# A hybrid decoder layer on one core: order of the first loads and products, the engine of the low parts, a buffer for attention's last piece, transposes one step ahead, gates and table loads moved

## The chip, the cores and the metric

The kernel runs on one core of one Trainium2 chip. The time is the device time of one execution in microseconds (us); several runs are made, and their median is compared. Engines are named as the profile names them: PE (TensorE), DVE (VectorE), ACT (ScalarE), POOL (GpSimd), SP (SyncE, which here issues nearly all DMAs).

## What is computed

One layer: a norm, one projection of 1024 to 2816 columns that is cut into eight parts, three groups of heads (a diagonal complex state-space scan with GELU and a sigmoid gate, a short convolution, attention into 256 memory tokens), one output projection, a residual sum and a final norm. Sequence 2048, model width 1024, all float32.

```python
hn = _rmsnorm(h, norm_g[l])
proj = hn @ w_in[l]
(a_in, a_gate, c_in, c_b, c_c, c_gate, q, q_gate) = jnp.split(proj, split_idx, axis=-1)
y_ssm = _s5_group(a_in, ...) * jax.nn.silu(a_gate)
y_conv = _short_conv_group(c_in, c_b, c_c, ...) * jax.nn.silu(c_gate)
mem_n = _rmsnorm(mem, mem_norm_g[l])
y_mem = _memory_xattn_group(q, mem_n, w_mem_kv[l]) * jax.nn.silu(q_gate)
y = jnp.concatenate([y_ssm, y_conv, y_mem], axis=-1)
h = h + y @ w_out[l]
...
return _rmsnorm(h, final_norm_g)
```

## The kernel before

**Products in three terms.** Each operand of a large product is kept as a high part, rounded to the matrix engine's float format (`fp32r`), and a low part, what rounding left. `mm3` (its three products are lines 81, 82 and 83) adds high x high, high x low and low x high. `split` makes the parts: ACT casts the high part (line 86), and the engine that it is given subtracts for the low part (line 77, the helper `tt`). So each weight tile costs a DMA, an ACT cast, and a subtraction of 128x1024 on DVE or POOL. `wtile` does all three; its default engine is POOL (`e=G`). `proj` passes DVE, but POOL for the tile q = 2; `wout` passes POOL, and `memory_kv` takes the default. `put` and `fetch_y` give some low parts of results to POOL too, and `glu` a sum. The staging buffers of weights (`wst`) are two, so a third load waits until a cast and a subtraction are done.

**Stages.** The sequence is cut into four tiles q of 512 columns. `prep` loads four row blocks of x, sums squares (ACT), scales rows (`row_rstd` with a power on POOL, then DVE, line 602), transposes them on PE (`rows_T`, names `trq`) and splits them into `hn`. `ain`, `agate`, `qproj` and `conv` are the eight parts of the projection, 24 products of 128x512 for each 128 columns (names `psai`, `psag`, `psq`, `psqg`, `psci`, `pscc`, `pscb`, `pscg`). `ssm_prologue`, `gen_table` and `gen_turns` build the state-space tables during tile 0 and write them to DRAM; `ssm` reads them back two buffers at a time (`tb`) and does `ps_v`, a scan on DVE, and `ps_y`. `memory_kv` makes keys and values (`psk`, `psv`). `attention` does scores (`sps`), exponents on ACT (`pe`), transposes (`trp`), their split (`pT`, line 77) and the weighting (`po`, line 809). `glu` gates the state-space result, `outproj` and `outproj_last` do the output projection (`po<-wo`) and the final norm.

**Order.** The program interleaves generators with fixed rates (end of the listing), and a scheduler then reorders each engine's instructions by its own estimate, save where the program forbids it. Each engine runs its queue in order; so an instruction that waits holds up all behind it. The order in which the engines got the instructions is shown with the change.

**Lines that matter.** L602 row scaling of x, L427 to L431 the table product and its sum and copy (`Kp`), L501 and L511 the table's load and `ps_v`, L619 `gate2` (`uq`, `ua`, `uc`), L783 scores, L790 exponents, L805 to L819 the rest of attention, L131 weight loads.

```python
for h in range(2):
    ...
    for mt_ in range(2):
        ...
        split(pT[:, 0], pT[:, 1], pt.rearrange("p i c -> p (i c)"))
        for z in range(2):
            T.matmul(po, vd[:, z, mt_, 2 * j + h], pT[:, z], start=mt_ + z == 0, stop=mt_ + z == 2)
```

## Time and profile before

| | |
|---|---|
| median of 3 runs | 890.51 us (889.22 to 893.97) |
| profiled execution | 893.49 us |
| its span, first to last instruction | 891.7 us |
| mean granted clock of PE | 0.980 |
| busy PE / DVE / ACT / POOL | 834.0 / 595.1 / 391.2 / 194.3 us |
| DMA | 142.88 MB, mean 160 GB/s |

The span is that of one execution under the profiler; 1.8 us lie around it. Busy time is the time in which an engine works on instructions; PE's products overlap and their ends are modelled. An engine's idle time is put down to what released it: `psqg L81 <- DVE uq L619` reads as the product of line 81 into `psqg`, which went on when DVE had made `uq` in line 619. The granted clock is 1.00 at 2.4 GHz and 0.50 at 1.2 GHz; a stretch's mean lies between.

### The profile page before, as it was taken

What the parts mean: (1) busy time and instruction counts of PE and PEld (TensorE: products, weight loads), DVE (VectorE), ACT (ScalarE), POOL (GpSimd) and SP (SyncE); (2) the same over time, 40 slices, a digit from 0 to 9 for tenths busy, and PEclk for the clock granted to TensorE, in tenths of its full rate; (3) what the DMA queues carried; (4) which work ended last, traced back from release to release, by engine and by line L of the source; (5) the groups of instructions that cost most, each with busy time, mean ns of one, the idle gap of its engine ahead of it and who ended that gap; (6) DMA issues with size and microseconds to landing.
All of it is one profiled execution on the core that took longest, in us unless ns stands there. A gap on an engine that the chain in (4) does not pass through costs nothing. (4 is left out here: it accounts for less than half of the span.)

```text
span 891.7 us, 11628 instructions
## 1 busy us (share of the span) xinstructions
PE 834.0 (94%) x4132; PEld 685.9 (77%) x4132; DVE 595.1 (67%) x1216; ACT 391.2 (44%) x758; POOL 194.3 (22%) x113
## 2 busy tenths in 40 slices
PE   2999899869997999999999989999999999998996
PEld 1986687767886888888888867888888888776885
DVE  5898799484798597855513584426478987785363
ACT  5243433354465446534434555334354336542511
POOL 2000001130000010344435553342000011265510
PEclk9999899999998999999999999999999999999998
DMA  9563646778566342384584743466747754486361
GB/s 202 148 172 95 184 132 190 205 202 238 167 183 195 100 130 78 103 210 134 141 263 121 197 111 97 119 191 208 213 135 206 209 158 119 125 209 186 98 189 47
DMA packets 170850, 142.88 MB, mean 160 GB/s; under 512 B 41128, under 2 KB 146600, under 8 KB 170792
## 3 DMA queue, kind: packets, MB, share of 16 engines
q1 hardware_dynamic: 170792, 142.14, 56.6%
q8 instruction: 32, 0.52, 0.2%
q14 instruction: 26, 0.21, 0.1%
HBM read 113.80 MB, written 26.74 MB: 158 GB/s over the span
## 5 line engine op out<-in xcount | busy, mean ns | idle before, releaser
L77 POOL TENSOR_TENSOR wo<-wo_st,wo 128x1024 fp32r<-128x1024 f32 x26 | 66.1, 2541 | 51.8 <-ACT wo L86 50.0
L86 ACT CAST wo<-wo_st 128x1024 fp32r<-128x1024 f32 x27 | 28.2, 1045 | 40.3 <-DMA wo_st<-in_w_out_dram 16.8
L81 PE MATMUL psai<-hn,wai 128*128 128x512 f32 (+1 forms) x120 | 42.4, 361 | 2.6 <-ACT hn L86 1.6
L82 PE MATMUL psai<-hn,wai 128*128 128x512 f32 (+1 forms) x120 | 42.6, 356 | 0.1
L83 PE MATMUL psai<-hn,wai 128*128 128x512 f32 (+1 forms) x120 | 42.3, 354 | 0.0
L81 PE MATMUL psag<-hn,wag 128*128 128x512 f32 x96 | 39.3, 409 | 0.0
L81 PE MATMUL pscg<-hn,wcg 128*128 128x512 f32 x96 | 38.7, 403 | 0.0
L83 PE MATMUL pscb<-hn,wcb 128*128 128x512 f32 x96 | 37.7, 392 | 0.9 <-DVE wcb L77 0.9
L81 PE MATMUL psci<-hn,wci 128*128 128x512 f32 x96 | 38.4, 400 | 0.0
L82 PE MATMUL psag<-hn,wag 128*128 128x512 f32 x96 | 38.4, 400 | 0.0
L82 PE MATMUL pscg<-hn,wcg 128*128 128x512 f32 x96 | 38.3, 399 | 0.0
L81 PE MATMUL pscb<-hn,wcb 128*128 128x512 f32 x96 | 38.2, 398 | 0.0
L83 PE MATMUL pscg<-hn,wcg 128*128 128x512 f32 x96 | 38.2, 397 | 0.0
L81 PE MATMUL pscc<-hn,wcc 128*128 128x512 f32 x96 | 38.1, 397 | 0.0
L83 PE MATMUL psag<-hn,wag 128*128 128x512 f32 x96 | 38.0, 396 | 0.0
L83 PE MATMUL pscc<-hn,wcc 128*128 128x512 f32 x96 | 37.7, 393 | 0.3 <-DVE wcc L77 0.3
L83 PE MATMUL psci<-hn,wci 128*128 128x512 f32 x96 | 37.8, 394 | 0.0
L82 PE MATMUL psci<-hn,wci 128*128 128x512 f32 x96 | 37.6, 391 | 0.0
L82 PE MATMUL pscc<-hn,wcc 128*128 128x512 f32 x96 | 37.5, 391 | 0.0
L77 POOL TENSOR_TENSOR ymem<-uq,ymem 128x512 fp32r<-128x512 f32 x4 | 5.2, 1296 | 148.3 <-DMA wcg_st<-in_w_in_dram 132.9
L82 PE MATMUL pscb<-hn,wcb 128*128 128x512 f32 x96 | 37.5, 391 | 0.0
L77 DVE TENSOR_TENSOR hn<-trq,hn 128x512 fp32r<-128x512 f32 x32 | 21.4, 683 | 23.3 <-ACT hn L86 23.3
(704 smaller groups left out, 2582.2 us busy)
## 6 DMA issues: line engine op xcount, KB each, us to landing
wo_st<-in_w_out_dram SPq DMA_DIRECT2D x32, 512.0 KB, 3.8
tb<-t_dram SPq DMA_DIRECT2D x16, 960.0 KB, 6.1
out_dram<-h SPq DMA_DIRECT2D x32, 256.0 KB, 3.6
h<-in_x_dram SPq DMA_DIRECT2D x14, 512.0 KB, 7.2
wai_st<-in_w_in_dram SPq DMA_DIRECT2D x12, 512.0 KB, 4.2
wag_st<-in_w_in_dram SPq DMA_DIRECT2D x12, 512.0 KB, 3.9
wci_st<-in_w_in_dram SPq DMA_DIRECT2D x12, 512.0 KB, 4.1
wcc_st<-in_w_in_dram SPq DMA_DIRECT2D x12, 512.0 KB, 4.0
```

Source lines behind the costliest of these rows:

```text
L77: e.tensor_tensor(o, a, b, op)
L81: T.matmul(ps, lh, rh, start=first, stop=False, **kw)
L82: T.matmul(ps, lh, rl, start=False, stop=False, **kw)
L83: T.matmul(ps, ll, rh, start=False, stop=last, **kw)
L86: S.copy(hi, src)
```

## The change

- **Start.** `first` replaces tile 0's `prep` and its part of `ain`. Rows 0 and 1 of x come first (half of row block 0 issued from ACT), then the three weight tiles as one buffer in three loads, then rows 2 and 3 into the weights' staging buffers. `norm_g` comes as 4 KB and is spread over partitions by two products with ones. The three accumulators are filled side by side, k by k, first the columns of rows 0 and 1.
- **Low parts.** `wtile`, `wout`, `put`, `fetch_y` and the sum in `glu` use DVE; POOL keeps the powers of the row scaling and some settings of memory.
- **Row scaling** with fewer steps: sums of two halves and factors are folded into other steps. `Dg` is added to the table product by PE (24 products of 16x16 more), and one ACT copy takes it out.
- **Tables** are requested at the head of the loop over b, one step ahead. **Gates** of the query (`qgate`) come behind `agate`. Loads of the memory rows, and the first transpose of some rows, keep the program's order.
- **Attention** transposes and splits one quarter ahead of its weighting; `um` is a buffer of its own.

```diff
-    def wtile(src, rows, cols, name, e=G, dst=None, stage="w"):
+    def wtile(src, rows, cols, name, e=V, dst=None, stage="w"):
...
-        V.tensor_scalar(v, ss, 1.0 / DM, EPS, ALU.mult, ALU.add)
+        if s1 is None:
+            V.tensor_scalar(v, s0, EPS * DM, None, ALU.add)
+        else:
+            V.scalar_tensor_tensor(v, s0, EPS * DM, s1, ALU.add, ALU.add)
...
-        tt(r2, r, a, ALU.mult)
+        V.scalar_tensor_tensor(r2, r, math.sqrt(DM), a, ALU.mult, ALU.mult)
...
+                T.matmul(kp[:NH, g, 0:NH], B1[:, b * GB + gg, :], R0[:, b * GB + gg, :], start=True, stop=False)
+                T.matmul(kp[:NH, g, 0:NH], ident[:NH, :NH], Dg[:, b * GB + gg, :], start=False, stop=True)
...
-            tt(Kp[:, xs_, 7 * NH:8 * NH], kp[:NH, :, 0:NH], Dg[:, b * GB + 3 * x_:b * GB + 3 * x_ + 3, :], ALU.add)
-            V.tensor_copy(Kp[:, xs_, 8 * NH:], kp[:NH, :, NH:])
+            S.copy(Kp[:, xs_, 7 * NH:], kp[:NH])
...
         for b in range(NS):
+            if b + 1 < NS:
+                table(b + 1)
...
             if b + 1 < NS:
-                table(b + 1)
                 vmm(b + 1)
...
+    def first():
...
+        xt = [xst.tile([P, DM], F32, tag="x", name=f"x0{i}") for i in range(2)]
+        xt += [wst.tile([P, DM], F32, tag="ws", name=f"x0{i}") for i in range(2, 4)]
+        wstg = stab.tile([P, KT, WS], F32, tag="tb", name="wai_st")
...
+        ks = ((0, 2), (2, 4), (4, 8))
...
+        nc.sync.dma_start(xt[0][0:NCH], xq[0, 0, :, 0])
+        nc.scalar.dma_start(xt[0][NCH:P], xq[0, 1, :, 0])
+        for z in range(2):
+            nc.scalar.dma_start(ngr[z], norm_g[0:1, halves[z]])
+        load_x(xt[1], 0, 1)
+        for a, b in ks:
+            nc.sync.dma_start(wstg[:, a:b], w_in[0, a * P:b * P, C_AIN:C_AIN + WS].rearrange("(k p) n -> p k n", p=P))
+        load_x(xt[2], 0, 2)
...
+            T.matmul(pb, ones, ngr[z], start=True, stop=True)
+            S.copy(ng_b[:, halves[z]], pb)
...
+        def mms(z, a, b):
+            o = slice(z * 256, z * 256 + 256)
+            for k in range(a, b):
+                for t in range(3):
+                    mm3(pss[t][:, o], wa[t][:, 0, k], wa[t][:, 1, k], hn[:, 0, k, o], hn[:, 1, k, o], k == 0, k == KT - 1)
...
+        yield from rows(0)
+        yield from rows(1)
+        for a, b in ks:
+            wsplit(a, b)
+        mms(0, 0, 2)
...
+        yield from rows(3)
+        mms(1, 0, KT)
...
-        w = wtile(w_in[0, :, c0:c0 + P], DM, P, f"w{nm}{q}", G if q == 2 else V)
+        w = wtile(w_in[0, :, c0:c0 + P], DM, P, f"w{nm}{q}")
...
-        put(q, "conv", t, u_, G if t < 2 else V)
+        put(q, "conv", t, u_)
...
+        um = late["um"].tile([P, QL], F32, tag="um", name=f"um{q}{j}")
...
+        turn(0, 0)
+        yield
+        turn(0, 1)
+        weigh(0, 0)
+        yield
+        turn(1, 0)
+        weigh(0, 1)
...
-            tt(g2, f32(y_ssm[:, 0, m, :]), f32(y_ssm[:, 1, m, :]), ALU.add, G)
+            tt(g2, f32(y_ssm[:, 0, m, :]), f32(y_ssm[:, 1, m, :]), ALU.add)
...
-    def wout(q, nh, kp, dst=None, st="w", e=G):
+    def wout(q, nh, kp, dst=None, st="w"):
...
-    for _ in weave(chain(agate(0), qproj(0), conv(0, 0), conv(0, 1)), side, 1.5):
+    for _ in weave(chain(agate(0), qproj(0), qgate(0), conv(0, 0), conv(0, 1)), side, 1.5):
...
-        return chain(qproj(q), agate(q), conv(q, 0), conv(q, 1), conv(q, 2))
+        return chain(qproj(q), agate(q), qgate(q), conv(q, 0), conv(q, 1), conv(q, 2))
```

`turn(h, mt_)` does the four transposes and the split of one quarter, `weigh(h, mt_)` its two products into `po` (line 872) and, with the second, the copy and the sum into `um`.

**Order on DVE at the start**, before: the halves of row 1 (`trq_0_231`, `trq_1_238`) and, behind them, `bg`.

```order
L77 TENSOR_TENSOR hn_183<-trq_0_231,hn_183 128x4x128
L77 TENSOR_TENSOR q03a<-q03r 128x1
L77 TENSOR_TENSOR q02a<-q02a,q02v 128x1
L77 TENSOR_TENSOR wai_169<-wai_st,wai_169 128x1024
L209 TENSOR_SCALAR j_en<-j_ex 128x24
L77 TENSOR_TENSOR hn_183<-trq_1_238,hn_183 128x4x128
L77 TENSOR_TENSOR q03a<-q03a,q03v 128x1
L96 TENSOR_SCALAR q02a<-q02a 128x1
L77 TENSOR_TENSOR s_Dg<-ident,j_dd 16x384
L124 TENSOR_SCALAR bg<-bg 128x3
```

And in the change, where row 1's first half is `trq_0_226`:

```order
L95 SCALAR_TENSOR_TENSOR q02v<-ssq_363 128x1
L214 TENSOR_SCALAR j_en<-j_ex 128x24
L95 SCALAR_TENSOR_TENSOR q03v<-ssq_500 128x1
L77 TENSOR_TENSOR s_Dg<-ident,j_dd 16x384
L127 TENSOR_SCALAR bg<-bg 128x3
L215 TENSOR_SCALAR j_en<-j_en 128x24
L77 TENSOR_TENSOR q02a<-q02r 128x1
L216 TENSOR_SCALAR j_ep<-j_en 128x24
L219 SCALAR_TENSOR_TENSOR j_er<-j_en,j_ex 128x24
L77 TENSOR_TENSOR q02a<-q02a,q02v 128x1
L217 TENSOR_SCALAR j_ebits<-j_ep 128x24
L77 TENSOR_TENSOR hn_144<-trq_0_226,hn_144 128x4x128
```

The two steps that need the small loads `dd` and `bg` now stand ahead of row 1's halves.

**Order on DVE at the last row of tile 1** (row block 3, scaled in the step `xb<-xb,q13o,ng_b`; `wai` are weights of the next projection), before:

```order
L77 TENSOR_TENSOR q13o<-q13r,q13a 128x1
L77 TENSOR_TENSOR wai_2152<-wai_st,wai_2152 128x1024
L77 TENSOR_TENSOR vd<-psv_1891,vd 128x2x64
L77 TENSOR_TENSOR vd<-psv_1965,vd 128x2x64
L602 SCALAR_TENSOR_TENSOR xb_1775<-xb_1775,q13o,ng_b 128x1024
L77 TENSOR_TENSOR hn_1774<-trq_0_1951,hn_1774 128x4x128
L77 TENSOR_TENSOR hn_1774<-trq_1_1958,hn_1774 128x4x128
L77 TENSOR_TENSOR wai_2222<-wai_st,wai_2222 128x1024
```

And in the change:

```order
L77 TENSOR_TENSOR hn_1805<-trq_0_1979,hn_1805 128x4x128
L77 TENSOR_TENSOR hn_1805<-trq_1_1986,hn_1805 128x4x128
L100 SCALAR_TENSOR_TENSOR q13o<-q13r,q13a 128x1
L77 TENSOR_TENSOR wai_2254<-wai_st,wai_2254 128x1024
L77 TENSOR_TENSOR vd<-psv_1993,vd 128x2x64
L658 SCALAR_TENSOR_TENSOR xb_1806<-xb_1806,q13o,ng_b 128x1024
```

The third `wai` (`wai_2222` before, `wai_2254` now) has come from behind the row to ahead of it.

**Order on PE at the second attention piece of tile 1 and the tables** (stretch of 278 us), before:

```order
L548 MATMUL ps_y_2854<-sC_2796,tb_2719 128x128
L783 MATMUL sps_2632<-kd,qh_2415 128x256 x6
L783 MATMUL sps_2633<-kd,qh_2415 128x256 x6
L511 MATMUL ps_v_2934<-pg_2802,tb_2932 128x128 x3
L547 MATMUL ps_y_2938<-pg_2802,tb_2805 128x128
L805 MATMUL trp_2775<-ident,pe_2486 128x128 x2
L805 MATMUL trp_2845<-ident,pe_2486 128x128 x2
L81 MATMUL psag_2816<-hn_1774,wag_2813 128x512
```

And in the change, where the row of `psqg` is the last of 21 that stand there:

```order
L83 MATMUL psqg_2850<-hn_1805,wqg_2847 128x512
L842 MATMUL sps_2668<-kd,qh_2451 128x256 x6
L842 MATMUL sps_2669<-kd,qh_2451 128x256 x6
L81 MATMUL psci_2910<-hn_1805,wci_2907 128x512
L82 MATMUL psci_2910<-hn_1805,wci_2907 128x512
L83 MATMUL psci_2910<-hn_1805,wci_2907 128x512
L81 MATMUL psci_2910<-hn_1805,wci_2907 128x512
L507 MATMUL ps_v_2841<-pg_2818,tb_2821 128x128 x3
L544 MATMUL ps_y_2889<-pg_2600,tb_2698 128x128
```

Projections now stand between scores, `ps_v` and `ps_y`.

## Rows read from the trace of the kernel before

**Rows 1.** The page, busy time of PE, share of the span, instructions.

```profile
PE 834.0 (94%) x4132; PEld 685.9 (77%) x4132; DVE 595.1 (67%) x1216; ACT 391.2 (44%) x758; POOL 194.3 (22%) x113
```

**Rows 2.** PE's waits, whole span: total us, times, longest us.

```profile
PE psqg L81 <- DVE uq L619: 4.5, 1, 4.5
...
PE psv L82 <- POOL wv L77: 3.4, 1, 3.4
PE trq L144 <- DVE xb L602: 3.3, 1, 3.3
PE po L82 <- POOL wo L77: 3.0, 3, 1.2
PE sps L783 <- ACT pe L790: 3.0, 1, 3.0
PE ps_v L511 <- DMA tb<-t_dram: 2.9, 1, 2.9
PE po L81 <- DVE h L77: 2.3, 1, 2.3
PE psk L83 <- POOL wk L77: 1.9, 1, 1.9
PE po L809 <- DVE pT L77: 1.8, 2, 1.2
PE po L809 <- ACT pT L86: 1.8, 1, 1.8
```

**Rows 3.** Busy time by stretch: PE, PEld, DVE, ACT, POOL, PEclk, DMA share, GB/s.

```profile
90.00:167.00 77.00, 74.22 (x349) 60.71 (x350) 63.70 (x131) 25.81 (x38) 5.24 (x4) 0.96 0.57 163
167.00:205.00 38.00, 28.26 (x169) 24.26 (x167) 26.79 (x57) 20.64 (x42) 10.60 (x6) 0.87 0.88 237
...
275.00:300.00 25.00, 19.09 (x93) 16.17 (x93) 18.01 (x39) 12.28 (x33) 0.00 (x0) 0.80 0.38 107
...
380.00:500.00 120.00, 119.93 (x557) 98.19 (x556) 55.93 (x74) 51.19 (x92) 58.08 (x28) 1.00 0.59 168
500.00:530.00 30.00, 26.40 (x115) 20.93 (x114) 21.02 (x31) 16.92 (x37) 15.29 (x9) 0.94 0.65 171
...
776.00:818.00 42.00, 38.49 (x165) 30.32 (x163) 32.76 (x28) 17.95 (x28) 28.55 (x14) 1.00 0.65 178
```

**Rows 4.** Timeline of DVE at the start: start us, us, instruction, idle before, releaser.

```profile
26.76 0.17 DVE L124 TENSOR_SCALAR bg<-bg 128x3 f32<-128x3 f32 x1 [1.48 <-DMA bg<-in_b_glu_dram]
```

**Rows 5.** The page's costliest groups, the cast of output weights: busy us, mean ns.

```profile
L86 ACT CAST wo<-wo_st 128x1024 fp32r<-128x1024 f32 x27 | 28.2, 1045 | 40.3 <-DMA wo_st<-in_w_out_dram 16.8
```

**Rows 6.** Timeline of DVE, 168 to 175 us.

```profile
171.04 2.23 DVE L653 SCALAR_TENSOR_TENSOR ycv<-ue,cw,ycv 128x512 f32<-128x512 f32 x1 [9.01 <-ACT ycv L652]
...
174.19 1.21 DVE L77 TENSOR_TENSOR wcg<-wcg_st,wcg 128x1024 fp32r<-128x1024 f32 x1
```

**Rows 7.** Timeline of POOL, key and value weights.

```profile
170.37 2.36 POOL L77 TENSOR_TENSOR wk<-wk_st,wk 128x1024 fp32r<-128x1024 f32 x1 [12.51 <-ACT wk L86]
...
184.59 3.97 POOL L77 TENSOR_TENSOR wv<-wv_st,wv 128x1024 fp32r<-128x1024 f32 x1
```

**Rows 8.** Timeline of DVE at the last row of tile 1.

```profile
199.08 1.27 DVE L602 SCALAR_TENSOR_TENSOR xb<-xb,q13o,ng_b 128x1024 f32<-128x1024 f32 x1
...
202.33 1.23 DVE L77 TENSOR_TENSOR wai<-wai_st,wai 128x1024 fp32r<-128x1024 f32 x1 [0.78 <-ACT wai L86]
```

**Rows 9.** DVE's groups, 776 to 818 us: busy us, mean ns, idle before, releaser.

```profile
L850 DVE SCALAR_TENSOR_TENSOR gt<-gt,gt 128x512 f32<-128x512 f32 x4 | 5.0, 1240 | 2.6 <-POOL gt L77 2.6
L77 DVE TENSOR_TENSOR yssm<-us,yssm 128x512 fp32r<-128x512 f32 x3 | 4.9, 1661 | 1.4 <-ACT yssm L86 1.4
...
L77 DVE TENSOR_TENSOR yssm<-ua,yssm 128x512 fp32r<-128x512 f32 x3 | 2.1, 684 | 0.1
```

**Rows 10.** Timeline of DVE, end of the first half of the output projection.

```profile
817.89 1.23 DVE L77 TENSOR_TENSOR hy<-wo_st,hy 128x1024 fp32r<-128x1024 f32 x1 [4.51 <-ACT hy L86]
819.04 1.88 DVE L77 TENSOR_TENSOR h<-po,h 128x512 f32<-128x512 f32 x3
```

**Rows 11.** DMA issues, 270 to 290 us: KB each, median us to landing.

```profile
tb<-t_dram SPq DMA_DIRECT2D x1, 960.0 KB, 8.1
```

161 lines of the change are left out of this document (89 added, 72 removed).

## The prediction

> **What bounds the kernel now.** The busy times come first: TensorE (PE) works 834.0 of 891.7 us [rows 1]. It is the bound, and what is left is its idle time and the time in which it runs at a lower clock. The list of PE's waits [rows 2] says what ended the idle time. Apart from the first loads, the reader is to see that no single engine is behind it: VectorE (DVE) `uq` 4.5, GpSimd (POOL) `wv`, `wo` and `wk` 3.4 + 3.0 + 1.9, DVE `xb` 3.3, ScalarE (ACT) `pe` 3.0, the load of `tb` 2.9, DVE `h` 2.3, and the transposed weights `pT` 1.8 + 1.8. These make 27.9 us. The third view gives the granted clock by stretch [rows 3]. Behind the longer waits PE falls from 2.4 to 1.2 GHz for some us, although it is busy again: the mean is 0.96, 0.87, 0.80 and 0.94 in the first, second, third and fifth stretch shown. Length times the missing share gives 3.1 + 4.9 + 5.0 + 1.8 = 14.8 us lost. So waits and clock together hold some 43 us; a change that only takes these away cannot bring more.
>
> The sum is made against the profiled execution, 893.5 us with 1.8 us around the span. It lies 3.0 us above the median of the three runs, 890.5; I take the same difference off it.
>
> **The start.** The change loads rows 0 and 1 of x, then the first weights in three pieces, then rows 2 and 3; it spreads `norm_g` over the partitions by two products instead of a broadcast load. PE's first projection products wait for both halves of row 1. Before, these stood on DVE ahead of `bg`, so DVE's wait of 1.48 us for the load of `bg` at 26.76 [rows 4] came behind them. Now `lam`, `ldt`, `dd` and `bg`, small loads that SP issues after all of x and the weights, stand ahead of these halves. I count that wait as exposed, 1.5 us. All three accumulators now end together, so the weights of the next projection can no longer be split while the last accumulator fills: one cast of 1.05 us [rows 5] and one low part of 1.21 us [rows 6] come on the path; 1.3 us go off it, the small waits between weights and rows that the k-by-k order hides. Together **+2.5 us**; bounds -1 (the new order hides everything) and +5 (the last small load lands 2.5 us later than I take).
>
> **The table prologue, to 92 us.** PE waits 4.5 us for `uq`, which stands on DVE behind the first tables' arithmetic, then loses 3.1 us at the low clock. The change takes the `Kp` sum and copy off DVE (one ACT copy instead) and with them DVE's waits for PE's `ps_k`. DVE reaches the gate some 4 us sooner, and PE, which comes later from the start, waits about 1 us and keeps its clock: **-6.5 us**, bounds -7.6 (all) and -3 (half the wait and the low clock stay). The price is 24 products of 16x16. From 380 to 500 us 557 products keep PE busy for 119.93 us [rows 3], 0.22 each, most of them of 512 columns; I take at most half of that for a small one, and part of them beside waits: **+1 us**, bounds 0 and 2.6.
>
> **Low parts off POOL.** POOL's 54 subtractions of 128x1024 and 26 of 128x512 go to DVE. At a key weight POOL takes 2.36 us, at a value weight 3.97 [rows 7]; DVE does such a piece in 1.21 [rows 6]. DVE also loses by the present arrangement: beside POOL's `wk` a 128x512 step with two SBUF inputs takes DVE 2.23 us [rows 6, 7], where undisturbed ones take 0.68 [rows 9]. So each moved piece costs DVE 1.21 and frees it of up to 1.5.
>
> The Trainium skill, "Perfetto Trace Analysis", section "Optimizing Scalar/DVE Operations", speaks against this part: the two engines share a read port of SBUF, so that moving work between them might not help. The rows just named agree that one engine holds up the other, but not that nothing is gained, since the same piece is half as long on DVE; by that rule the two terms that rest on it, keys and output projection, would be nil, and the sum -16.5 us.
>
> Most moved pieces lie between 380 and 650 us. From 380 to 500 DVE is busy 55.9 of 120 us beside 28 POOL steps [rows 3]. At 1.21 these add at most 34 us to DVE, which makes 75%. PE does not wait there now.
>
> *Keys, values, second x tile (167 to 205).* PE waits 1.9 + 3.4 + 3.3 and loses 4.9 by the clock [rows 2, 3]. The low parts end 1.1 and 2.7 us sooner. But the last wait is for row 3 of x, which DVE normalised at 199.08, and only at 202.33 did it take the low part of the third `wai` [rows 8]. In the new order on DVE that low part stands **ahead** of the row. With loads where they were, the row would begin at 203.56, 4.5 us later; but the weights' loads wait for buffers, which DVE now releases sooner than POOL did, by 1.1 and 2.7 us at the two pieces above. These nearly cancel: PE arrives sooner and waits longer. **-2.5 us**, bounds -8 (the waits for `wk` and `wv` go, with most of the low clock) and +4.5.
>
> *Output projection (776 to 818).* The waits for `wo`, 3.0 us, go, for DVE splits sooner than POOL. DVE is busy 32.8 of 42 us here beside 14 POOL steps [rows 3], six of 1.21 and eight of 0.68 us, 12.7 together. It gets back what is stretched beside POOL: the seven steps of the first two groups shown hold 9.9 us where 0.68 each would make 4.8 [rows 9], and other groups are stretched too. So it stays under 41 of 42. The 2.3 us for `h` came from DVE's queue: it sat 4.51 us for the weights of `hy` with three sums `h` behind [rows 10]. Now three of the four sums stand ahead of it. **-4 us**, bounds -5.3 and -1.
>
> **Tables one step ahead, projections between.** At 278 PE does scores, `ps_v` and `ps_y` with no projection between, waits 3.0 for `pe` and 2.9 for `tb`, and loses 5.0 by the clock, 10.9 us in all [rows 2, 3]. In the new order 21 products of `psqg` (some 4.6 us at the 0.22 above) stand ahead of those scores and four of `psci` ahead of `ps_v`. The table's load took 8.1 us from issue here [rows 11]. There are still only two buffers, so the load begins when the earlier table's last reader is done, some 7 us of PE work ahead of its need. I leave 2 us: **-9 us**, bounds -10.9 and -3 (load and clock loss stay in part).
>
> **Transposes one step ahead.** Around 513 to 526 PE waits three times for `pT`, 3.6 us, with 1.8 lost by the clock. The transposes of the next quarter now stand ahead of each weighting, with projection products between; the sum `um` has its own buffer. A split of 128x512 takes DVE 0.68, which five or more products cover. **-4.5 us**, bounds -5.4 and -2.
>
> The merged steps of the row scaling, the earlier loads of the memory rows and the moved gates change no time by themselves: PE's projections of 24 products cover them, and without this cover they would show as one low part, 1.21. Nil.
>
> **Sum.** +2.5 - 6.5 + 1 - 2.5 - 4 - 9 - 4.5 = -23 us: 870.5 for a profiled execution, **867 us** (890.5 less 23, rounded) for the median. All bounds at their best give -38, 852; all at their worst +3, 894.
>
> **Rivals.**
> 1. *The gaps only move* (20%). The third `wai` keeps row 3 back, the tables still land late, and the clock falls once after each. The start at +5, keys at +2, tables at -4, the rest as above: -11, 879.5. For it: the DVE order at row 3, the two table buffers. Against it: PE's order has projections in the place of each old gap.
> 2. *Tables are not really earlier* (8%): issued a step ahead in the program, but held by their buffer until where they were. The 2.9 and most of the clock loss at 278 stay; -16, 874.5. The change would then not do what it says.
> 3. *POOL's work costs DVE as much as it cost POOL* (7%), the shared port as a mechanism of this kernel: DVE's two-input steps were slow by their own demand. Keys and output projection bring nothing, -16.5, 874. Against it: 0.68 beside 2.23 for steps of one size.
> 4. *DVE's queue becomes what POOL's was* (5%), **slower**. Every low part waits on DVE for its load, with everything behind it. The trace has the price: 4.51 us of DVE for one late load, 2.3 us of PE [rows 2, 10]. If 10 of the 54 new pieces meet it, the gain is gone; from 12 on the kernel is slower beyond noise; at 14, +32 - 23 = +9, 900 us. It decides wherever loads land later than DVE's other work is due. Against it: DVE has half its time free where most of the pieces lie.
>
> **Chances.** The forecast's own case, 854 to 876, has 56%; another 4% lies below it. About 0.5% (4.5 us) is what measurement can tell from no change. Faster: nearly all of the forecast's case, and most of rivals 1 to 3, 87%. Within 0.5%: their poor ends, 8%. Slower 5%. The range reaches from 853 (nearly all bounds at their best) over rivals 1 to 3 to 884; beyond it lie the poorest part of rival 1, rival 4, and too great a gain.
>
> **What would show it.** Right: no releaser on POOL among PE's waits but the row scaling; clock 1.00 around 92, 290 and 518; DVE without steps of 2 us for 128x512; the first gate projection some 2 us later than before. Wrong: PE waits behind DVE steps that are themselves waiting for weights, a wait for `tb` of over 2 us, or a first projection that starts 5 us late.

## The result: 885.6 us, a third of the forecast gain

Six runs of each kernel gave medians of 885.6 us for the changed kernel (884.8 to 888.5) and 892.6 us for the one before (889.2 to 894.2): a ratio of 0.9932, interval 0.9906 to 0.9958. A second measurement (e9) gave 884.1 against 893.2, 0.9904 (0.9883 to 0.9925). So the change gains 0.7 to 1.0%, where 2.6% was forecast, and the time lies 1.6 us above the forecast's range. The profiled span is 883.0 us (891.7 before), the mean clock 0.979 (0.980).

The busy line of the page after, which answers to [rows 1]:

```profile
PE 844.2 (96%) x4184; PEld 691.6 (78%) x4184; DVE 608.5 (69%) x1266; ACT 397.3 (45%) x774; POOL 21.1 (2%) x33
```

POOL is nearly empty, as meant. PE's idle time fell by 19 us, and the span by only 8.7: PE is busy 10 us longer. 3.8 of these are work at 1.2 GHz (29.8 us of busy time at that clock, 25.9 before), and some are added products; the rest was not taken apart. PE's waits after (total us, times, longest us), which answer to [rows 2]:

```profile
PE ngb L601 <- DMA ngr<-in_norm_g_dram: 5.5, 1, 5.5
PE trq L147 <- issue: 4.6, 1, 4.6
PE psg L81 <- ACT gt L922: 3.0, 2, 2.6
PE tr_b L190 <- DMA j_bo<-in_ssm_b_re_dram: 2.8, 1, 2.8
PE ps_k L431 <- DVE hn L77: 2.5, 1, 2.5
...
PE trq L147 <- ACT gt L425: 1.7, 1, 1.7
PE psai L82 <- DVE hn L77: 1.5, 1, 1.5
```

None of PE's waits for POOL, `pT` or `wo` is left; of those for `tb` and `pe` 1.1 and 0.5 us are (below the lines shown). New are, beside `ngb` (the products that spread `norm_g`) in the first microseconds, `psg` (the product of the state path's gate), `tr_b` (the transposes of B) and `ps_k`. Busy time by stretch after, with columns as in [rows 3] (PE, PEld, DVE, ACT, POOL, granted clock, DMA share, GB/s):

```profile
44.00:56.00 12.00, 8.36 (x35) 6.02 (x34) 8.83 (x34) 7.02 (x19) 0.00 (x0) 0.86 0.63 162
86.00:100.00 14.00, 14.00 (x83) 9.68 (x82) 10.40 (x37) 7.23 (x14) 1.10 (x2) 0.76 0.42 100
185.00:216.00 31.00, 25.68 (x149) 20.76 (x149) 20.78 (x44) 19.43 (x51) 0.73 (x1) 0.72 0.77 216
276.00:296.00 20.00, 18.87 (x104) 15.31 (x104) 15.95 (x36) 10.28 (x28) 0.00 (x0) 1.00 0.44 129
500.00:530.00 30.00, 29.86 (x140) 24.39 (x139) 21.24 (x38) 16.66 (x31) 2.49 (x2) 1.00 0.63 171
766.00:776.00 10.00, 7.36 (x26) 5.56 (x25) 7.84 (x11) 5.49 (x8) 0.00 (x0) 0.83 0.92 205
776.00:818.00 42.00, 41.37 (x181) 33.51 (x180) 31.82 (x45) 20.30 (x30) 0.00 (x0) 1.00 0.55 172
```

And the same view of the kernel before, for stretches that [rows 3] don't have:

```profile
44.00:56.00 12.00, 12.00 (x56) 9.63 (x56) 10.43 (x46) 7.30 (x22) 0.00 (x0) 1.00 0.82 204
86.00:100.00 14.00, 9.48 (x40) 6.90 (x38) 10.89 (x42) 5.51 (x9) 1.10 (x2) 0.76 0.67 166
185.00:216.00 31.00, 24.27 (x145) 19.89 (x145) 21.90 (x46) 14.55 (x32) 4.35 (x2) 0.89 0.74 201
766.00:776.00 10.00, 9.08 (x44) 7.28 (x43) 9.70 (x16) 7.96 (x12) 1.68 (x1) 1.00 0.50 141
```

The stalls at 278 and 513 us are cured (clock 1.00, PE nearly full), and so are the waits after 776. New losses are the stretches at 44, at 185 and at 766; at 86 PE no longer waits but runs at the low clock.

**A ledger by work done.** Stretches of two kernels at one time hold different work. So I laid the traces side by side by work: each product counts what it takes at 2.4 GHz in the trace (0.2265 us for 512 columns), and the products that the change adds count nothing. The attention scores, two of which run beside each other, count next to nothing in it, in all kernels alike. All kernels here have 780.6 us of work. The *lag* at a point is the time when PE gets there, less the work up to there; what a stretch adds to it is what waits, clock and added products cost there. Growth of the lag against the kernel before, in us, by stretches of work (my arithmetic from the traces), with the single parts of experiments e5 to e7 beside it:

```
work, us                         forecast  changed  e5 low   e6 tables  e7 transp.
0-30    start                      +2.5     +7.2     -0.6     +0.6       -1.5
30-130  first tables, prologue     -5.5     -1.1     +0.6     +0.2       +0.1
130-210 keys, values, x tile 2     -2.5     -0.5     +5.8     -0.4       +0.3
210-230 stall at 278 us            -9.0     -9.1     -0.4    -10.5       -5.6
230-430                             0       +1.5     -1.2     +0.6       +0.1
430-470 stall at 513 us            -4.5     -5.4     -5.8     +0.8       +0.2
470-680                             0       -0.1     -1.3     -0.4       -0.5
680-690 768 us in the changed       0       +4.5      0        0          0
690-720 output projection          -4.0     -5.3     -6.1     -1.2       +2.3
rest                                0       -0.4      0.0     +0.3       -0.1
total                             -23.0     -8.7     -9.0    -10.0       -4.7
```

Each column is one profile, and so is the kernel before. The changed kernel profiled a second time (e9) has +9.6 at the start and +3.2 at 768 us; its other lines lie within 1.5 us of those shown. So a line by itself is good to some 2 us.

### The profile page after: what moved, and what is told of

Same layout as the page of the kernel before. It is cut to its first block, busy times and chain, and to the rows that moved or that the text cites. A ratio compares the mean times of both kernels' runs of the same rounds, so it can differ in the third digit from the quotient of the medians.

```text
span 883.0 us, 11661 instructions
## 1 busy us (share of the span) xinstructions
PE 844.2 (96%) x4184; PEld 691.6 (78%) x4184; DVE 608.5 (69%) x1266; ACT 397.3 (45%) x774; POOL 21.1 (2%) x33
## 5 line engine op out<-in xcount | busy, mean ns | idle before, releaser
L77 DVE TENSOR_TENSOR wo<-wo_st,wo 128x1024 fp32r<-128x1024 f32 x27 | 33.0, 1222 | 29.0 <-ACT wo L86 28.9
L82 PE MATMUL psai<-hn,wai 128*128 128x512 f32 (+1 forms) x120 | 43.4, 362 | 1.7 <-DVE hn L77 1.5
L81 PE MATMUL psai<-hn,wai 128*128 128x512 f32 (+1 forms) x120 | 43.0, 368 | 0.7 <-ACT hn L86 0.7
L83 PE MATMUL psai<-hn,wai 128*128 128x512 f32 (+1 forms) x120 | 42.7, 356 | 0.0
L849 ACT ACTIVATE pe<-sps,nm 128x256 f32<-128x256 f32 x64 | 29.7, 476 | 20.8 <-DVE nm L847 20.7
L81 PE MATMUL pscg<-hn,wcg 128*128 128x512 f32 x96 | 37.9, 394 | 0.0
L83 PE MATMUL pscg<-hn,wcg 128*128 128x512 f32 x96 | 37.8, 393 | 0.0
L82 PE MATMUL pscg<-hn,wcg 128*128 128x512 f32 x96 | 37.6, 392 | 0.0
L81 PE MATMUL po<-wo,yssm 128*128 128x512 f32 x84 | 32.9, 396 | 0.8 <-ACT yssm L86 0.8
```

What stands on the lines that cost most here:

```text
L77: e.tensor_tensor(o, a, b, op)
L81: T.matmul(ps, lh, rh, start=first, stop=False, **kw)
L82: T.matmul(ps, lh, rl, start=False, stop=False, **kw)
L83: T.matmul(ps, ll, rh, start=False, stop=last, **kw)
L849: S.activation(pe[:, a, h], sps[h][:, a], AF.Exp, bias=nm_[:, a, h:h + 1], accum_out=sm[:, a, h:h + 1])
```

## The experiments

All kernels compute the whole layer. Medians, with the kernel before on the same chip; the kernels between two bars shared a chip. Ratios are to the kernel before; spans are of one profiled execution.

```
                          median   before   ratio   interval          span
e1  small steps on POOL   883.15   895.54   0.9862  0.9840 to 0.9883  880.0
e2  + two B buffers       877.79   895.54   0.9799  0.9775 to 0.9823  872.2
e3  Dg on DVE             878.83   895.54   0.9818  0.9795 to 0.9840  879.1
e4  residual late         886.95   895.54   0.9913  0.9891 to 0.9934  884.9
-----
e5  low parts only        885.05   894.39   0.9895  0.9874 to 0.9916  882.7
e6  tables ahead only     884.47   894.39   0.9888  0.9865 to 0.9911  881.7
e7  transposes only       890.60   894.39   0.9959  0.9940 to 0.9979  887.0
e8  repairs joined        881.25   894.39   0.9852  0.9827 to 0.9877  876.8
-----
e9  changed kernel again  884.13   893.20   0.9904  0.9883 to 0.9925  884.2
e10 start and residual    874.63   893.20   0.9800  0.9773 to 0.9828  868.7
e11 rows in po            874.77   893.20   0.9807  0.9783 to 0.9830  872.5
e12 Dg on GpSimd          871.37   893.20   0.9758  0.9734 to 0.9781  868.7
-----
e13 third weight on POOL  889.83   893.35   0.9955  0.9938 to 0.9972  889.7
e14 value weights on POOL 884.14   893.35   0.9888  0.9866 to 0.9910  882.9
e15 e12 + e13's edit      870.96   893.35   0.9743  0.9718 to 0.9768  869.3
e16 e12 + e14's edit      872.76   893.35   0.9758  0.9736 to 0.9779  871.0
-----
e17 e16, attention slower 874.73   895.17   0.9770  0.9746 to 0.9795  872.8
e18 e16, projections more 879.33   895.17   0.9824  0.9799 to 0.9848  875.7
```

### The start: e1 and e2

e1 moves the small steps that wait for small loads from DVE to POOL; PE's and ACT's orders stay as in the changed kernel.

```diff
-        V.tensor_scalar_mul(bg, bg, 0.5)
+        G.tensor_scalar_mul(bg, bg, 0.5)
-            V.tensor_copy(lamn[:, :, :, d, :], lam_.rearrange("g z (k i) -> g z k i", k=4))
+            G.tensor_copy(lamn[:, :, :, d, :], lam_.rearrange("g z (k i) -> g z k i", k=4))
-        expf(dt, ldt)
+        expf(dt, ldt, G)
```

> The changed kernel, with the four small steps that wait for the late small loads (the two copies of lam, the first step on log_dt, Dg, the halving of bg) moved from VectorE's queue to GpSimd's. TensorE's order stays as it was. Theory: at the start the changed kernel loses 3.0 us because VectorE waits 1.37 us for lam and 1.67 us for bg ahead of row 1's scaling and of row 1's halves; without them TensorE's first projection products begin 3 us sooner (halves of row 1 at about 20 instead of 23.0 us) and the whole is 3 us shorter than the changed kernel, 2 at least. Rival: the order of the first products by k is what costs, and VectorE's waits lie beside another that ends as late (weights, row 1's casts on ScalarE); then the first products move by under 1 us and the time by under 1 us.

DVE's timeline of the changed kernel (start us, us, instruction, idle before with its releaser) shows two waits ahead of row 1, where I had priced one:

```profile
17.70 0.35 DVE L196 COPY j_lamn<-j_lam__294 24x128 f32<-24x128 f32 x2 [1.37 <-DMA j_lam__294<-in_ssm_lam_im_dram]
18.66 1.39 DVE L612 SCALAR_TENSOR_TENSOR x<-x,q01o,ng_b 128x512 f32<-128x512 f32 x2
...
22.42 0.17 DVE L127 TENSOR_SCALAR bg<-bg 128x3 f32<-128x3 f32 x1 [1.67 <-DMA bg<-in_b_glu_dram]
23.03 0.68 DVE L77 TENSOR_TENSOR hn<-trq,hn 128x512 fp32r<-128x512 f32 x1
```

In e1 neither is there:

```profile
17.00 1.40 DVE L612 SCALAR_TENSOR_TENSOR x<-x,q01o,ng_b 128x512 f32<-128x512 f32 x2
...
20.32 0.68 DVE L77 TENSOR_TENSOR hn<-trq,hn 128x512 fp32r<-128x512 f32 x1
```

Row 1's half comes 2.7 us sooner, and the lag at 30 us of work falls from 33.1 to 30.0. 1.37 + 1.67 = 3.0 us is the price of the two waits.

e2 adds a second buffer for the state-space matrix B, whose second load had to wait until the first copy was used:

```diff
-            for bd, (s1, s2) in ((b1, (b_re, b_im)), (b2, (b_im, b_re))):
+            for bd, bo, (s1, s2) in ((b1, bo, (b_re, b_im)), (b2, bo2, (b_im, b_re))):
```

> As the first kernel of this set, and the two layouts of the state matrix B loaded into two buffers instead of one after the other into the same. Theory: the 2.8 us that TensorE waits for the second load at 48 us, with two products of the next projection done, go, and with them the 3.4 us at 1.2 GHz behind it, 1.7 us lost; 4.5 us less than the first kernel of this set, 6 to 8 less than the changed kernel. Rival: the wait passes to the next load in line (the matrix C, the next weights) or the clock falls there without it: 0 to 1.5 us less than the first.

PE's wait `tr_b` of 2.8 us is gone, with the low clock behind it (44 to 56 us: busy 11.32 where the changed kernel has 8.36, and 1.00 where it has 0.86):

```profile
44.00:56.00 12.00, 11.32 (x50) 8.47 (x49) 10.60 (x25) 6.35 (x10) 0.00 (x0) 1.00 0.66 197
```

The lag at 30 falls by another 3.6 us to 26.4, 0.5 above the kernel before. So the start costs 7.2 us in the changed kernel, and all but 0.5 of it is these two things. It holds in other profiles too: the start costs 7.2 to 9.6 us in the six that have the changed one, and -0.4 to +0.5 in the nine that have e2's.

### The 24 small products: e3

The addition of `Dg` goes back from PE to DVE, and the copy of `Kp` from ACT to DVE; everything else is the changed kernel.

```diff
-                T.matmul(kp[:NH, g, 0:NH], ident[:NH, :NH], Dg[:, b * GB + gg, :], start=False, stop=True)
...
-            S.copy(Kp[:, xs_, 7 * NH:], kp[:NH])
+            tt(Kp[:, xs_, 7 * NH:8 * NH], kp[:NH, :, 0:NH], Dg[:, b * GB + 3 * x_:b * GB + 3 * x_ + 3, :], ALU.add)
+            V.tensor_copy(Kp[:, xs_, 8 * NH:], kp[:NH, :, NH:])
```

> The changed kernel, with the sum of Dg and the copy of Kp back on VectorE as before the change, so without the 24 products of 16x16 and the copy on ScalarE. Theory: the run of small products at 88 to 96 us, which these 24 lengthen, is what lets the clock fall at 91.8 us with TensorE busy; without them TensorE has 2.8 us less work and the clock stays up or falls for half as long, 3 to 6 us less in this stage, and VectorE's waits for the products bring back up to 4.5 us at the gate, so that the whole is 4 us faster to 1 us slower. Rival: VectorE's place in the chain is what counts; the gate's wait comes back in full with the low clock behind it, as before the change, and the whole is 2 to 6 us slower than the changed kernel.

The stretch that ran at 0.76 with PE busy all of its 14 us now runs at full clock, though PE has waits in it:

```profile
86.00:100.00 14.00, 13.03 (x76) 8.97 (x75) 10.71 (x45) 6.82 (x13) 1.06 (x2) 1.00 0.34 74
392.00:412.00 20.00, 17.50 (x75) 14.21 (x74) 10.14 (x16) 6.06 (x11) 0.55 (x1) 0.91 0.41 119
```

From 30 to 130 us of work the lag grows by 1.5 us instead of 6.1 (7.2 before): 4.6 us for 24 products (48 instructions in the trace, two for each), of which 14 x 0.24 = 3.4 is the clock. It is no accident of one run: the clock fell between 86 and 100 us in all nine kernels here that have the new order and these products, and in none of the seven that have the new order without them. Against the kernel before, the nine gain 0.2 to 1.2 us from 30 to 130 us of work, the seven 5.8 to 7.0. It is the products and neither ACT's copy nor another order of PE: e12 (below) keeps that copy, and apart from these products PE's order is that of the changed kernel in e3 up to 101 us, and that of e11 in e12 up to 104 us. In e12:

```profile
86.00:100.00 14.00, 14.00 (x70) 11.08 (x69) 10.09 (x25) 8.35 (x15) 1.64 (x4) 1.00 0.66 164
```

Part of e3's gain is given back at 392 us (second row above): PE waits 2.5 us for DVE's sums `h`. Why these come late was not isolated; e13 and e14, which keep the products, have the same wait, so it does not come of the place of `Dg` alone.

### The load of the residual rows: e4 and e10

At 768 us PE waits for `psg`. ACT's timeline, then SP's, of the changed kernel:

```profile
769.51 0.62 ACT L86 CAST yssm<-gr 128x512 fp32r<-128x512 f32 x1 [2.59 <-DMA gr<-g_dram]
770.03 0.68 ACT L922 ACTIVATE gt<-psg,bg 128x512 f32<-128x512 f32 x1
```

```profile
759.92 1.30 SPq L972 DMA_DIRECT2D h<-in_x_dram  x2
761.33 0.53 SPq L910 DMA_DIRECT2D gr<-g_dram  x1
```

`gr` is a piece of the state path's result, read back from DRAM. Here its load stands behind 1 MB of residual rows `h`. In the kernel before, these loads are issued at 782.12, since their buffer also held attention's sum `um`. With `um` in its own buffer it is free 22 us sooner; in e7, where only attention is changed, they start at 762.62. But the buffer alone does not make the wait: in e7 these loads stand behind three of the tile's four pieces `gr`, in the changed kernel behind one, and in e7 PE has no wait for `psg` (it loses 2.3 us more than before at 690 to 720 us of work). Why the pieces stand later in the changed kernel was not isolated. There the cast waits 2.59 us, the gate `gt` stands behind it, and PE's `psg` behind that. e4 issues the loads of this tile behind the second pair of output weights:

```diff
-        h = residual(q)
+        h = residual(q) if q != 3 else None
...
+                if h is None and kp == pairs[1]:
+                    h = residual(q, keep=True)
```

> The changed kernel, with the loads of the 2 MB of x for the last but one output projection's sum issued after the loads of the state path's gate instead of ahead of them; nothing else moves before 755 us. Theory: these 2 MB, which in the changed kernel start at 760 us, hold up the 256 KB piece that ScalarE casts (it waits 2.6 us for it), the gate's tanh stands behind that cast, and TensorE waits 2.6 us for the tanh and then runs 3.4 us at 1.2 GHz; with the order turned the wait at 768 us and the low clock go, 4 to 5 us less. Rival: the sum's loads now come too late, the accumulators wait for VectorE's sums, and TensorE waits as long some 20 us on: within 1.5 us of the changed kernel, or slower.

PE's waits in e4 from 755 to 820 us, and one of ACT's:

```profile
PE po L81 <- ACT yssm L86: 4.2, 1, 4.2
PE psg L81 <- ACT gt L922: 1.3, 1, 1.3
```

```profile
ACT wo L86 <- DMA wo_st<-in_w_out_dram: 5.0, 1, 5.0
```

The wait moved: from 773.99 the 2 MB stand ahead of the output weights, ACT waits 5.0 us for these, and PE 4.2 for what ACT has behind them. e4's span is 884.9 us, no shorter than the changed kernel's (883.0, and 884.2 in e9). So the cause was right and the repair wrong: one block of 2 MB held up something at both places where it stood. e10 splits it, on top of e2: half behind the first pair, half behind the third.

```diff
+                if q == 3 and nh == 0 and kp in (pairs[0], pairs[2]):
+                    z = len(h)
+                    h.append(late["big"].tile([P, 2, DM], F32, tag=f"big{z}", name=f"h{q}{z}"))
```

> The kernel of the two buffers for B (which has the small steps on GpSimd), and the 2 MB of x for the next to last projection in two halves, the second after the last pieces of the state path; TensorE's order up to 750 us is that of the kernel of the two buffers. Theory: the wait of 3 us for the gate's tanh and the low clock behind it go, and with half of the 2 MB at each place no other wait over 1.5 us takes their place: 3 to 5 us less than the kernel of the two buffers, ratio to the kernel before 0.975 to 0.977. Rival: the 2 MB have no quiet place in this stage, the wait passes on to a weight or a state piece 20 us later as in e4: within 1.5 us of the kernel of the two buffers, 0.979 to 0.981.

The lag between 680 and 700 grows by 2.7 us (e2: 6.2; a wait for `psg` of 2.0 us is left), and the span falls from 872.2 to 868.7, each that of the fastest run of its kernel. The ratios, 0.9800 against e2's 0.9799 on other chips, do not resolve these 3.5 us; only the traces show them.

### The parts alone, on the kernel before: e5, e6, e7

e5 moves the low parts from POOL to DVE and nothing else:

```diff
-    def wtile(src, rows, cols, name, e=G, dst=None, stage="w"):
+    def wtile(src, rows, cols, name, e=V, dst=None, stage="w"):
...
-            split(Y[q][part][:, 0, t, :], Y[q][part][:, 1, t, :], u_, e)
+            split(Y[q][part][:, 0, t, :], Y[q][part][:, 1, t, :], u_)
```

> The kernel before, with nothing changed but the engine of the low parts: VectorE takes every subtraction that GpSimd had. Theory (the forecast's terms for this part): about 2.5 us come back around the keys and values and 4 us in the output projection at 776 to 818 us, nothing is lost elsewhere; 5 to 8 us less than before. Rival one, the shared port as the bound: VectorE's steps stay as long as they were and the time stays within 1.5 us. Rival two, VectorE's queue: its low parts wait for late weights with everything behind them, and the time is over 2 us longer.

It gains 9.0 us by the ledger, in two places: the output projection (-6.1) and, not foreseen, the stall at 513 us (-5.8). There the kernel before has on DVE and POOL:

```profile
513.92 2.38 DVE L642 COPY ue<-ue 128x126 f32<-128x126 f32 x1
```

```profile
513.66 2.55 POOL L77 TENSOR_TENSOR wci<-wci_st,wci 128x1024 fp32r<-128x1024 f32 x1 [0.22 <-POOL yconv L77]
```

and e5, with nothing on POOL beside it:

```profile
514.63 0.22 DVE L642 COPY ue<-ue 128x126 f32<-128x126 f32 x1
```

A copy of 0.22 us takes 2.38 beside a step of POOL and ends with it; the split of `pT` stood behind it, at 516.29. From 495 to 525 us PE is in e5 busy all 30.00 us (27.01 before). That this copy is the whole of the stall is argued from these rows; e5 moves every low part at once. What the move costs DVE shows in the busy line of e5's page:

```profile
PE 833.2 (94%) x4132; PEld 687.7 (78%) x4132; DVE 613.9 (70%) x1296; ACT 392.6 (44%) x758; POOL 18.7 (2%) x33
```

The 80 steps that DVE takes over are worth 83.0 us at 1.21 and 0.68 each, and DVE is busy only 18.8 us longer than before (595.1, [rows 1]). The other 64 us it gets back from its own steps, which no longer run beside POOL's. But keys, values and the second x tile get 5.8 us worse. PE's waits for POOL there, 3.4 + 1.9 us [rows 2], are replaced by waits for DVE's rows and their splits (`ps_k` 3.1, `trq` 1.6, `sps` 1.6, `tr_m` 1.3), and from 185 to 216 us the clock is 0.72 where the kernel before has 0.89.

e6 requests tables one step ahead and puts the query's gate behind `agate`:

```diff
+            if b + 1 < NS:
+                table(b + 1)
...
-        return chain(qproj(q), agate(q), conv(q, 0), conv(q, 1), conv(q, 2))
+        return chain(qproj(q), agate(q), qgate(q), conv(q, 0), conv(q, 1), conv(q, 2))
```

> The kernel before, with the loads of the state path's tables one step ahead and the query gate's projections moved from behind the queries to behind the attention gate, and nothing else. Theory: at 278 us the 10.9 us of waits and low clock go down by 9 and the gain stays to the end, 7 to 10 us less than before. Rival: without the other parts VectorE is late at the same place (its share there is smaller, but GpSimd's low parts are still slow), half of the waits stay, 3 to 5 us less.

The stall at 278 us is gone whole (in the kernel before PE is busy 19.09 of 25 us there, at 0.80 [rows 3]). Which of the two moves cures it was not separated. In e6:

```profile
270.00:295.00 25.00, 25.00 (x130) 20.15 (x129) 21.59 (x47) 14.17 (x36) 0.00 (x0) 1.00 0.62 181
```

e7 is attention alone, transposes one quarter ahead and `um` in its own buffer:

```diff
+        turn(0, 0)
+        yield
+        turn(0, 1)
+        weigh(0, 0)
```

> The kernel before, with attention's transposes one quarter ahead of the weighting and the sum in a buffer of its own, and nothing else. Theory: 5 us come back around 513 to 526 us; and since the sum no longer holds the buffer of the scores, the 2 MB of x for the next to last projection start some 20 us sooner (760 instead of 782 us) and hold up the state path's pieces, which costs up to 5 us at about 775 us; in all between 5 us less and no change. Rival: the early 2 MB are harmless by themselves and the stall at 768 us of the changed kernel comes from the low parts on VectorE; then 5 us less and no wait for the gate's tanh.

It does nothing at 513, where I had put its gain. PE's waits from 495 to 525 us, and DVE's copy:

```profile
PE po L813 <- ACT pT L86: 1.6, 1, 1.6
PE po L813 <- DVE pT L77: 1.4, 1, 1.4
```

```profile
507.23 2.38 DVE L642 COPY ue<-ue 128x126 f32<-128x126 f32 x1
```

Its -5.6 lies at 278 us, where its waits for `pe` and `tb`, 3.0 and 2.9 before, fall to 0.4 and none; 1.6 us for `sC` (made from the scan's result), are new. The three parts together would give -9.0 - 10.0 - 4.7 = -23.7 us, but e6 and e7 both take the 278 stall: 16.1 us between them, of 13.4 that the kernel before loses there.

### All repairs, and the second x tile: e8, e11 to e18

e8 joins e2, e3's edit and e10's two halves.

> The changed kernel with four repairs together: small steps of the start on GpSimd, two buffers for B, the sum of Dg on VectorE, and the 2 MB of x for the next to last projection in two halves, one after the first two pieces of the state path and one after its last. Theory: the repairs lie in different stages and add up: 3 at the start, 4 to 7 by the two buffers, 4 to 8 at the first tables, 2 to 5 at 768 us; 14 to 20 us less than the changed kernel, 864 to 871 on a chip where that takes 885. Rival: the order of the work shifts behind each repair and new waits open, as e3 showed with 2.5 us for the sums at 399 us; 8 to 12 us less.

The start and the prologue are cured (lag at 130: 26.7; changed 39.2), but the wait for `h` that e3 showed at 392 is longer, 3.9 us, and from 320 to 340 us of work the lag grows by 8.0 us. e12 takes `Dg` to POOL instead, on top of e11:

```diff
+            tt(Kp[:, xs_, 7 * NH:8 * NH], Kp[:, xs_, 7 * NH:8 * NH], Dg[:, b * GB + 3 * x_:b * GB + 3 * x_ + 3, :], ALU.add, G)
```

> As the kernel before it in this set, and the sum of Dg on GpSimd after ScalarE's copy of Kp, so without the 24 products of 16x16 and without VectorE's wait for the tables' products. Theory: as with the sum on VectorE (e3), the small products' 2.8 us go and the clock does not fall at 90 us: 4 to 5 us less than the kernel before it up to 120 us, and no wait comes back at the gate. Rival: the order of the later work shifts with it as in e3 and e8 (a wait for the sums at 399 us), which gives it back: within 2 us.

The lag at 130 is the same 26.8, and from 320 to 340 it grows by 0.6. Beside e9, the changed kernel on the same chip, e12 is 12.8 us faster (871.4 against 884.1).

> The changed kernel itself, on the same chip as the three kernels beside it, so that these can be compared with it directly. Both theories: ratio to the kernel before as in the first measurement, 0.993 within 0.003; lag behind by 7 us at the start, 17 us at 1.2 GHz around 200 us, and the wait for the gate's tanh at 768 us, all as before.

Left is the stretch at 185. e11 puts two row blocks of tile 1 into a buffer of their own in PSUM (where PE writes its results), so that `ps_k` need not wait for the rows' (on top of e10):

```diff
-                              *((ps_ss, "ss") if q == 1 and i % 2 else (ps_tr, "tr")))
+                              *((ps_tr, "tr") if q != 1 else (ps_ss, "ss") if i % 2 else (ps_po, "po")))
```

> As the kernel before it in this set, and in the second x tile the transposes of rows 0 and 2 go to the free PSUM buffer of the attention's output instead of the two that the tables' products use. Theory: the 4.1 us that TensorE waits ahead of the tables' second half at 188 us are a wait for a PSUM buffer, which VectorE's split of a transposed row holds, not for an operand; with another buffer the wait falls below 1.5 us and part of the 10 us at 1.2 GHz behind it goes: 3 to 7 us less than the kernel before it. Rival: row 3 of x, which VectorE scales late, is then what TensorE waits for, and the clock falls all the same: within 2 us.

The wait, 4.1 us in e2, is gone, and nothing is gained (e10 and e11 have the same median on one chip): PE is busy 29.86 of 31 us, still at 0.72 (first row). The price of that stretch is the clock, and it fell at 189 us after 24 us in which PE had no wait at all. e13 and e14 give one low part each back to POOL, e16 does e14's on top of e12 (second row):

```diff
-        w = wtile(w_in[0, :, c0:c0 + P], DM, P, f"w{nm}{q}")
+        w = wtile(w_in[0, :, c0:c0 + P], DM, P, f"w{nm}{q}", G if (q, nm) == (1, "ai2") else V)
```

```diff
-        wv = [wtile(w_mem_kv[0, hh * 512:(hh + 1) * 512, WM:2 * WM], 512, WM, f"wv{hh}") for hh in range(2)]
+        wv = [wtile(w_mem_kv[0, hh * 512:(hh + 1) * 512, WM:2 * WM], 512, WM, f"wv{hh}", G) for hh in range(2)]
```

```profile
185.00:216.00 31.00, 29.86 (x137) 23.03 (x136) 16.16 (x33) 15.07 (x37) 0.00 (x0) 0.72 0.72 206
```

```profile
185.00:216.00 31.00, 30.43 (x164) 23.16 (x162) 14.76 (x27) 17.74 (x44) 3.27 (x2) 1.00 0.87 255
```

> The changed kernel, with one low part, that of the third weight of the second x tile's first projection, back on GpSimd; TensorE's and VectorE's orders stay as they were up to some 190 us. Theory T1: row 3 of x stands on VectorE behind this low part, which waits 1.05 us for ScalarE's cast and takes 1.23; without it row 3 is scaled 2.3 us sooner (199.3 instead of 201.6 us), the first projection of this tile begins 2 us sooner and with it the clock rises a step sooner: 3 to 6 us less than the changed kernel. Theory T2: row 3 is not what the low clock hangs on; the wait gets shorter but the clock is down for 17 us as before, under 1.5 us less.

> The changed kernel, with the low parts of the two value weights back on GpSimd as before the change. Theory T2: the 48 large products with the values' weights then come later, among the transposes of x and of the tables, and the run of small products from 190 to 211 us is broken up; TensorE waits some 3 us longer for the weights, but the clock is at 1.2 GHz for 7 us or less instead of 17: 2 to 5 us less than the changed kernel at 220 us. Theory T1: the wait for the weights comes back and the low clock stays as long as it was, 2 to 4 us more than the changed kernel.

e13 tests my reading that the third `wai`, ahead of row 3 on DVE, is what keeps that row back. In the changed kernel it stands there and waits for its cast, and the row comes 2.5 us later than before (199.08 at [rows 8]):

```profile
200.27 1.23 DVE L77 TENSOR_TENSOR wai<-wai_st,wai 128x1024 fp32r<-128x1024 f32 x1 [1.05 <-ACT wai L86]
201.62 1.27 DVE L658 SCALAR_TENSOR_TENSOR xb<-xb,q13o,ng_b 128x1024 f32<-128x1024 f32 x1
```

But PE does not wait for it; it is busy with other work, at 1.2 GHz:

```profile
199.00:214.00 15.00, 15.00 (x73) 11.45 (x73) 6.92 (x12) 10.14 (x29) 0.00 (x0) 0.50 0.72 198
```

And e13 does not bring the row sooner: with the weight on POOL the row itself is stretched:

```profile
203.01 2.93 DVE L658 SCALAR_TENSOR_TENSOR xb<-xb,q13o,ng_b 128x1024 f32<-128x1024 f32 x1
```

```profile
202.51 2.35 POOL L77 TENSOR_TENSOR wai<-wai_st,wai 128x1024 fp32r<-128x1024 f32 x1 [10.88 <-ACT wai L86]
```

So e13 does not show what an earlier row would bring. Its longer span (889.7 us) is not lost here but at 392 us, where PE waits 3.1 us for `h` and the lag grows by about 6 us from 320 to 340 us of work (the changed kernel: next to nothing). In e14 the value products come later again and the clock rises from 0.72 to 0.78. By 230 us of work e14 has gained 3 to 4 us on the changed kernel's two profiles since 130, as its theory T2 said, and about 5 go again at 392 us, by the same wait for `h` (2.3 us); so the span stays.

> The fastest kernel so far (the sum of Dg on GpSimd, the start's small steps on GpSimd, two buffers for B, rows in the output's PSUM buffer, the 2 MB in two halves), with the third weight's low part on GpSimd. T1: 2 to 5 us less than that kernel, ratio to the kernel before 0.970 to 0.974. T2: within 1.5 us of it, 0.974 to 0.978.

> The same fastest kernel, with the value weights' low parts on GpSimd. T2: the 17 us at 1.2 GHz from 191 us go down to 7 or less and the wait of 2.4 us with them, 2 to 6 us less, ratio to the kernel before 0.969 to 0.974. T1: the wait for the weights is added, 2 to 4 us more, 0.978 to 0.981.

e15 and e12 can't be told apart. e16 has the stretch at 1.00 (its clock is down for 3.4 us from 177.9, behind a wait of 2.9 us, instead of 17.1), and its lag at 210 us of work is 9.4 us lower than e12's (40.8 against 50.3); at 320 it is 0.8 **higher** (61.2 against 60.4). e17 and e18 change the rates at which this stage's generators are interleaved:

```diff
-    interleave(main(1), merge(chain(ssm(0), glu(1)), att(1), 0.4), 3.4)
+    interleave(main(1), merge(chain(ssm(0), glu(1)), att(1), 0.34), 3.8)
```

(e18; e17 has 0.3 and 3.4.)

> The kernel of e16 with one number changed: in the second stage attention's steps are woven into the state path's at a rate of 0.30 instead of 0.40, so that 24 projection products stand between the state path's gate and the output projection. If the loss at 363 to 376 us in e16 is a wait of the order there: that loss of 10.6 us falls below 4, ratio to the kernel before 0.966 to 0.971. If the state path's chain sets the end of the stage: TensorE waits elsewhere in it, ratio 0.974 to 0.979.

> The kernel of e16 with two numbers changed: in the second stage attention at a rate of 0.34 instead of 0.40 and the other steps at 3.8 instead of 3.4 for each projection step. The same two expectations: 0.966 to 0.971 if the loss is a wait of the order there, 0.974 to 0.979 if the state path's chain sets the end of the stage.

Neither gains: spans of 872.8 and 875.7 us against 871.0, and lags of 63.4 and 63.9 at 320. In the nine kernels that have the start of e2 (e2, e8, e10 to e12, e15 to e18) the lag at 210 lies between 40 and 51 us, and at 320 between 59 and 64, with no relation between the two. So what is won at 185 us does not reach the end of this stage. I took the chain of tile 0's scan, table by table, for the cause; the traces of e12 and e16 do not show that. From 228 to 345 us PE is busy throughout in both, at full clock:

```profile
228.00:345.00 117.00, 117.00 (x637) 96.88 (x636) 103.30 (x222) 62.34 (x136) 0.00 (x0) 1.00 0.48 145
228.00:345.00 117.00, 116.91 (x626) 96.68 (x627) 98.27 (x211) 60.85 (x135) 0.00 (x0) 1.00 0.47 142
```

The first `ps_v` starts at 228.8 us in e12 and at 221.8 in e16, 7.0 us sooner; the `ps_v` of the last table at 321.6 and 323.0. Between the two PE does 83.3 us of work in e12 and 90.2 in e16. So the 7 us went into projections that now stand ahead of the state path in PE's order, and behind it PE waits 4.4 us for `yssm`, the state path's result. Why the scheduler places them so was not isolated.

## Why the prediction failed, step by step

Three places make up 13.6 of the 14.3 us between forecast and result: the start (4.7), the clock in the prologue (4.4) and a load at 768 us that the sum does not have (4.5).

- **The start** (+2.5, bounds -1 and +5): mis-sized, +7.2 and outside the bounds. The mechanism was there, a small load on DVE ahead of row 1. But I priced the one wait that the trace of before showed, and two other waits were the change's own: `lam` (1.37) beside `bg` (1.67), and behind them the one B buffer, 2.8 us of PE with the clock's loss (e1, e2: 3.1 and 3.6 us). What then is left, +0.5, answers the +1.0 that I had beside the wait.
- **The prologue** (-6.5 + 1): **the step that failed is "and keeps its clock"**. The wait for `uq` went as forecast; the clock fell all the same, now with PE busy throughout, because of the 24 products that I had priced at 1 us by their duration. They cost 4.6, by e3: 3.4 by the clock, at nothing in my sum, and 1.2 by themselves. The term came out at -1.1; in the seven kernels without them it is -5.8 to -7.0, about what I had forecast for it.
- **Keys, values, x tile 2** (-2.5, bounds -8 and +4.5): -0.5, and not by two waits that nearly cancel. Row 3 of x came later, as the order said (2.5 us, where I had up to 4.5), but PE, which was to wait for it, had other work and did not. The waits got shorter and the clock lower: alone, the low parts cost 5.8 us here (e5). e11 shows that a wait was not the price: with it gone the clock is as low as before. What makes the clock fall here stays open.
- **Tables** (-9): -9.1. Right, with projections in the gap; e6 alone takes the whole stall.
- **Transposes** (-4.5): -5.4. The size was right and the reason wrong. The gain belongs to the low parts (e5), since DVE was held up by POOL ahead of `pT` (argued from its rows); the new order alone leaves the stall (e7).
- **Output projection** (-4): -5.3, through the low parts, as said (e5 -6.1).
- **Not in the sum**: 4.5 us at 768. I noted that `um` gets its own buffer, and did not ask which load had been waiting for the old one. In e7 the early load alone does not stop PE there; it did with the other parts of the change.

Of my signs of being right all came but one: no wait for POOL, clock 1.00 at 290 and 518 us, no DVE step of 128x512 over 0.8 us (16 over 1.3 before), the first gate projection 2.7 us later; the clock at 92 us did not. Of the signs of being wrong none came as I had put it.

From the forecast to the result it is +4.7 (start), +4.4 (prologue), +2.0 (keys), +4.5 (768), -2.2 (513 and output projection) and +0.9 (the rest): 14.3 us, from -23 to -8.7.

Of the rivals, the first came nearest: 879.5, "the gaps only move". The start overshot its +5; its late tables did not come. Tables were really earlier (rival 2), and no DVE queue took POOL's place (rival 4). Rival 3 said nil for keys and output projection together. In e5 that number comes out, -0.3 (+5.8 and -6.1), but not by its mechanism: DVE got back 64 of the 83 us that it took over, and the output projection gained; the loss is at the low clock of the keys' stretch. In the changed kernel the two make -5.8. The Trainium skill ("Perfetto Trace Analysis", "Optimizing Scalar/DVE Operations") says that work moved between GpSimd and VectorE might not help because of the shared port. The rows agree on the sharing, 2.38 us against 0.22 for one copy; here it goes with a gain: with POOL's steps gone DVE's own got shorter (e5).

## What to carry to other kernels

Price added products on PE not by their duration but also by what they do to the clock: look at the granted clock of the stretch, as with the small ones here; a busy PE is no proof that the clock stays. When a tile gets a buffer of its own, find the load that was waiting for the old one: it can start sooner, ahead of whatever is needed there. And add up gains by stall, not by edit: two parts that cure one stall bring it once.

## What the runs showed of the hardware that was not expected

- The clock fell to 1.2 GHz with PE busy all the time: 0.76 for 86 to 100 us at 14.00 of 14.00 us in the changed kernel, 0.72 for 185 to 216 us at 29.86 of 31 in e11, and 1.00 at 30.43 of 31 in e16. In e11 the last 6 us ahead of the fall, from 183 us, hold 30 instructions into `ps_k` of 16 to 112 columns and 22 into `psv` of 256. At 86 us the runs show the cause (the products with `Dg`); at 185 us they don't.
- Some steps of DVE last until a step of POOL beside them ends: 2.38 us for a copy that takes 0.22 alone, 2.35 for the one-column step `q31a` (522.70 in the trace of before; 0.16 alone). Others do not: 16 sums `h<-po,h` beside POOL's steps took 0.68 us there, as alone. For a queue that works in order this matters more than the mean: what stood behind the copy was late by 2 us.
